# Untied differences of the gate weights, a place of its own for the first sums' split, spread puts, swapped PSUM pools and other turns of the late tiles in a float32 encoder layer

## Chip, cores and metric

One core of one Trainium2 chip runs the whole layer. The metric is the device time of one execution in microseconds (us). The engines are named as in the profile: PE is TensorE (matmul), DVE is VectorE, ACT is ScalarE, POOL is GpSimd, SP is SyncE, which issues most transfers (its queue shows as SPq).

## What is computed

A layer on 1024 tokens of width 1024, in float32, cut here to its skeleton:

```python
h = swiglu(rmsnorm(x, ffn1_pre_g), w_gate, w_up, w_down)      # 1024 -> 2816 -> 1024
x = x + 0.5 * rmsnorm(h, ffn1_post_g)
q, k, v = split(rmsnorm(x, mix_pre_g) @ w_qkv)                 # 16 heads of 64
o_na = neighbourhood_attention(q[:8], k[:8], v[:8], rel_bias)  # 2-D windows
o_dil = dilated_mixture_attention(q[8:], k[8:], v[8:], t5_bias)
mixed = concat(rmsnorm(o_na, na_out_g), rmsnorm(o_dil, dil_out_g)) @ w_out
x = x + rmsnorm(mixed, mix_post_g)
h = swiglu(rmsnorm(x, ffn2_pre_g), ...)                        # as above
x = x + 0.5 * rmsnorm(h, ffn2_post_g)
```

## The kernel before

**Products.** A float32 product is made of three matmuls on halves: `split` (L418 to L423) makes a high half on ACT (a cast, L421, names whi) and a low half on DVE (L422, wlo), and `mm3` (L325, L326, L327) multiplies high by high, high weight by low activation, low weight by high activation. Above that the large products follow a scheme with seven block products and pre-added operands: tiles are named A11, A12, A22 for plain quadrants and S1 to S4 for sums of the activations; T1, T2 and B22 are the weights' counterparts. One product of a block is four steps of three matmuls, 12 in all.

**Gate and up (`PairGemm`).** FFN 1 and FFN 2 each have 22 blocks of 128 columns; gate and up of a block form one such scheme. `ahead` first goes over the early blocks (9 in FFN 1, 10 in FFN 2) with the left half of the gate weights alone, while the last token tiles (4 to 7, the late tiles) are still normed, transposed and summed into S1 to S4; its results wait in DRAM. Then `run` takes all blocks in order. In an early block TensorE runs S2 with T2 (giving u2, L548), S1 with T1 (v, L556), S3 with T1 (c22, L575), S4 with B22, and one product later A22 with B22 (c21, L584). `prepare(b + 1)` gives the next block's weight work in four parts: `direct`, the differences on DVE (L510, L511, L512: first T1's pair, then T2, then B22's second); `second`, the split of T2; `sums`, the split of T1; `rest`, the split of B22 and the fetch of the block after (SP, L415 and L416). `begin` does `direct` and `second` for block 0 ahead of `run`, and `begin_rest` the others. The sink (`GatePairs`) applies silu and, after every second (odd) block, forms pair sums for the next product in four DVE operations (L647 to L650).

**Down, values.** `Passes` streams pairs of row blocks: raw tiles (praw, SP, L680 and L683), their halves (pw, L685 and L686), and the products accp. At the end of the last gate/up block, `final` closes the pools wg, tj and wt (T2's tiles) and opens on their space a pool for the first passes' four raw tiles. The q,k columns are a `PairGemm` with 8 blocks, all early, after the values' passes; its sink is `QKPairs`.

**Order.** TensorE's order is written out; on the other engines a scheduler orders by dependences and costs, except where `c.behind(f, engines)` ties what f issues behind the last instruction issued so far on those engines. Every engine works its own instructions in order. `plan` gives turns: `{1: [U(4)]}` has tile 4 put (transposed) from block 1's tick on.

**Other places.** Dilated heads read their queries regrouped by residue (`q_by_residue`, L978) and work scores (L1068, names sp), a fused add and sum on DVE (L989), exponentials on ACT (L991), transposes (L999) and values (L1089). The neighbourhood heads' output is normed in two quads of four token tiles (`scale`, L1237) and put: transposed by TensorE (L1248) and split (L1252, L1253), between the output projection's matmuls. `gemm_psum` opens the PSUM pools psm (6 banks of products) and pst (2 banks of transposes). A late tile runs through left_half and right_half (L260, L272 on ACT, L273 to L287 on DVE).

## Time and profile before

| what | before |
|---|---|
| median of three runs | 1915.44 us (1915.32 to 1922.39) |
| the profiled execution's own time | 1915.59 us |
| its span | 1913.4 us |
| TensorE busy | 1846.7 us, 97% |
| VectorE busy | 1331.3 us, 70% |
| ScalarE busy | 830.7 us, 43% |
| GpSimd busy | 318.7 us, 17% |
| mean granted TensorE clock | 0.993 |

Rows of the timeline give the start in us, the duration, the engine, line and operation, the tiles (out<-in, buffer numbers left out), the shape, and in brackets how long the engine stood idle before and what ended that. Rows of the waits give who waited for whom, then microseconds in all, times, and the longest. A transfer's landing is when its data is there, counted from its issue.

### The profile page before, as it was taken

Reading aid. Unit: us, or ns where it says so; the run is one execution under the profiler, and the core shown is the slowest. Engines: PE = TensorE matmul, PEld = TensorE weight load, DVE = VectorE, ACT = ScalarE, POOL = GpSimd, SP = SyncE. Lnnn points to the kernel's source line nnn. Section 1 sums busy time; section 2 is a strip of 40 time slices with the busy share of each in tenths; the row PEclk is TensorE's granted clock in tenths of the full one; section 3 lists DMA queues with packets and bytes.
Section 4 is the critical chain, followed back from the end, with each engine's and each line's share of the span. In section 5 each row is a group of like instructions: output and inputs, shape, how many; then the busy total and the mean of one; then the engine's idle time right before and its main releaser. Section 6 shows DMA issues by size and latency. Waiting matters only on the chain.

```text
span 1913.4 us, 25103 instructions
## 1 busy us (share of the span) xinstructions
PE 1846.7 (97%) x8904; PEld 1532.9 (80%) x8904; DVE 1331.3 (70%) x2233; ACT 830.7 (43%) x1491; POOL 318.7 (17%) x502
## 2 busy tenths in 40 slices
PE   7999999999999999899999999999999999999998
PEld 5777888888778877788899998877777888888886
DVE  6767777766565986467677756786768777654557
ACT  7422333334353656223588765563222333344333
POOL 2123111112210123122333100120101111110000
PEclk9999999999999999999999999999999999999999
DMA  7655565645996857757876432584546655476564
GB/s 264 220 182 192 166 237 209 227 158 201 342 330 197 287 194 257 253 165 236 281 234 224 166 136 89 183 307 143 174 151 231 218 194 210 157 267 217 195 227 146
DMA packets 171215, 404.94 MB, mean 212 GB/s; under 512 B 19841, under 2 KB 42273, under 8 KB 169042
## 3 DMA queue, kind: packets, MB, share of 16 engines
q1 hardware_dynamic: 123410, 243.18, 38.3%
q0 software_dynamic: 46672, 158.07, 22.9%
q10 hardware_dynamic: 1008, 2.10, 0.3%
q8 instruction: 70, 1.15, 0.2%
q14 instruction: 55, 0.45, 0.1%
HBM read 277.34 MB, written 130.99 MB: 213 GB/s over the span
## 4 chain that ended last, share of the span: by engine, by line
PE 64%; issue 16%; DVE 7%; DMA 6%; ACT 4%; POOL 2%; SPq 0%; DVEq 0%; POOLq 0%; ACTq 0%
PE mmp L327 11%; PE mmp L326 10%; PE mmp L325 10%; PE accp L326 8%; PE accp L327 8%; PE accp L325 8%; PE po L1089 2%; PE ptp L999 2%; PE po L1201 2%; DVE wlo L422 1%; PE sp L1068 1%; PE trp L157 1%; ACT whi L421 1%; PE sp L1185 1%; DVE pw L686 1%
## 5 line engine op out<-in xcount | busy, mean ns | idle before, releaser
L325 PE MATMUL mmp<-x,whi 128*128 128x512 f32 (+1 forms) x1464 | 579.9, 396 | 10.3 <-ACT whi L421 7.5
L327 PE MATMUL mmp<-x,wlo 128*128 128x512 f32 (+1 forms) x1464 | 576.9, 394 | 10.9 <-DVE wlo L422 10.9
L326 PE MATMUL mmp<-x,whi 128*128 128x512 f32 (+1 forms) x1464 | 574.9, 393 | 1.2 <-DVE x L244 0.7
L327 PEld LDWEIGHTS mmp<-x,wlo 128*128 128x128 f32 x1464 | 277.4, 189 | 76.5 <-DVE wlo L422 14.8
L325 PEld LDWEIGHTS mmp<-x,whi 128*128 128x128 f32 x1464 | 277.6, 190 | 74.2 <-ACT whi L421 12.0
L326 PEld LDWEIGHTS mmp<-x,whi 128*128 128x128 f32 x1464 | 277.4, 189 | 61.7 <-DVE x L244 1.0
L686 DVE TENSOR_TENSOR pw<-praw,pw 128x1024 fp32r<-128x1024 f32 (+1 forms) x181 | 201.6, 1158 | 128.8 <-ACT pw L685 128.5
L421 ACT CAST whi<-wraw 128x1024 fp32r<-128x1024 f32 x129 | 135.2, 1050 | 320.1 <-PE mmp L326 246.9
L685 ACT CAST pw<-praw 128x1024 fp32r<-128x1024 f32 (+1 forms) x181 | 168.9, 981 | 205.8 <-PE accp L327 144.6
L325 PE MATMUL accp<-pw 128*128 128x512 f32 x600 | 235.1, 392 | 2.1 <-ACT pw L685 1.1
L326 PE MATMUL accp<-pw 128*128 128x512 f32 x600 | 234.2, 390 | 1.8 <-DVE pw L686 1.8
L327 PE MATMUL accp<-pw 128*128 128x512 f32 x600 | 233.8, 390 | 0.0
L422 DVE TENSOR_TENSOR wlo<-wraw,whi 128x1024 fp32r<-128x1024 f32 x129 | 157.8, 1224 | 23.4 <-ACT whi L421 23.0
L325 PEld LDWEIGHTS accp<-pw 128*128 128x128 f32 x600 | 112.7, 188 | 27.5 <-ACT pw L685 2.4
L326 PEld LDWEIGHTS accp<-pw 128*128 128x128 f32 x600 | 112.7, 188 | 26.0 <-DVE pw L686 3.0
L327 PEld LDWEIGHTS accp<-pw 128*128 128x128 f32 x600 | 112.7, 188 | 23.2
L584 DVE TENSOR_TENSOR c<-mmp,u 128x512 f32<-128x512 f32 x52 | 36.0, 692 | 106.9 <-PE mmp L327 106.9
L630 POOL DMA_DIRECT2D g<-sg x44 | 23.9, 544 | 488.3 <-DVE sg L623 296.4
L440 ACT COPY s<-mmp 128x512 f32<-128x512 f32 x52 | 30.6, 588 | 127.1 <-PE mmp L327 118.6
L421 ACT CAST whi<-traw 128x512 fp32r<-128x512 f32 x52 | 32.3, 621 | 98.9 <-DVE traw L511 98.7
L510 DVE TENSOR_TENSOR wraw<-wraw 128x1024 f32<-128x1024 f32 x52 | 63.5, 1221 | 7.8 <-DMA wraw<-in_wqk_dram 7.0
L1201 PE MATMUL po<-vs,pt 128*128 128x128 f32 x352 | 50.1, 277 | 1.5 <-ACT pt L1001 1.1
(280 smaller groups left out, 2756.8 us busy)
## 6 DMA issues: line engine op xcount, KB each, us to landing
praw<-g SPq DMA_DIRECT2D x70, 512.0 KB, 5.6
wraw<-in_wg_dram SPq DMA_DIRECT2D x44, 512.0 KB, 4.2
wraw<-in_wu_dram SPq DMA_DIRECT2D x44, 512.0 KB, 6.0
tr<-in_wd_dram SPq DMA_DIRECT2D x44, 512.0 KB, 6.1
g<-sg POOLq DMA_DIRECT2D x88, 256.0 KB, 4.0
ts<-tr POOLq DMA_DIRECT2D x22, 1024.0 KB, 4.7
praw<-ts SPq DMA_DIRECT2D x88, 256.0 KB, 4.6
praw<-in_wd_dram SPq DMA_DIRECT2D x66, 256.0 KB, 5.3
```

The source lines that it names most:

```text
L325: nc.tensor.matmul(out, ahi, bhi, start=start, stop=False, skip_group_check=go_on)
L326: nc.tensor.matmul(out, ahi, blo, start=False, stop=False, skip_group_check=go_on)
L327: nc.tensor.matmul(out, alo, bhi, start=False, stop=stop, skip_group_check=go_on)
L421: nc.scalar.copy(hi, raw)
L422: nc.vector.tensor_sub(lo, raw, hi.bitcast(F32))
L510: nc.vector.tensor_sub(r[:, 0:2], r[:, 1:3], r[:, 0:2])
L584: nc.vector.tensor_add(c21, d, u2)
L685: nc.scalar.copy(hi, raw[:, :m])
L686: nc.vector.tensor_sub(lo, raw[:, :m], hi.bitcast(F32))
L999: nc.tensor.transpose(ps[:, j, :], src[:, j * P:(j + 1) * P], c.ident)
L1089: nc.tensor.matmul(po[:, un * 2 + j], pt[:, 2 * j + t, :], rhs, start=t == 0, stop=t == 1)
L1201: nc.tensor.matmul(po[0][:, u], pt[0][:, j, :], vs[:, k0 + j, :], start=j == 0, stop=j == n - 1)
```

## The change

It has these parts: `direct` is tied behind DVE only in `QKPairs` (`ties`), not in `GatePairs`; the split of T1 goes into the pool wt, and that of block 0 is issued in `begin` behind DVE and ACT, with the last early block's silu behind ACT; the q,k `begin` as a whole is issued behind DVE and ACT; the norm's squares of late tiles go behind ACT; the first pair of tiles in FFN 1's second half keeps its raw copy for later; the late tiles' turns in FFN 1 change; the first dilated head's queries are regrouped by ACT and not by GpSimd; the second quad of the neighbourhood heads is scaled tile by tile with the puts, and the eight puts stand at other distances between the matmuls; and FFN 2 opens pst ahead of psm.

```diff
     def norm(self, ts, xs):
-        n = self.squares(ts, xs)
+        n = []
+        self.c.behind(lambda: n.extend(self.squares(ts, xs)), ACT)
         self.c.sums.append(lambda: self.scale(*n))
...
+    def tied(self, f):
+        self.c.behind(f, *self.sink.ties)
...
         def sums():
-            w[T1] = self.split(r[:, 0:2, :], "m")
+            w[T1] = self.split(r[:, 0:2, :], "m", self.c.wt)
...
     def begin(self):
-        direct, second, *self.more = self.prepare(0)
+        direct, second, sums, *self.more = self.prepare(0)
         direct()
         second()
+        self.c.behind(sums, DVE, ACT)
...
-                c.behind(direct, DVE)
+                self.tied(direct)
                 second()
...
 class GatePairs:
+    ties = ()
...
-        nc.scalar.activation(sg, ps, AF.Silu)
+        c.behind(lambda: nc.scalar.activation(sg, ps, AF.Silu), *tie)
...
 class QKPairs:
+    ties = (DVE,)
...
-    def scale(self):
+    def scale(self, n=4):
...
+    def scaled(self, i):
+        o = self.og[:, self.b0 + i, :]
+        self.c.nc.vector.scalar_tensor_tensor(o, o, self.r[:, i:i + 1], self.gain, op0=ALU.mult, op1=ALU.mult)
...
-                        c.steps.extend(lambda t=t: op0.one(t) for t in (2 * b - 2, 2 * b - 1))
+                        c.steps.extend(lambda t=t: op0.one(t, *([keeps] if t > 1 else [])) for t in (2 * b - 2, 2 * b - 1))
...
-                                    {0: [F(4, 5), L(6, 7)], 1: [U(4), F(6, 7)], 2: [U(5)], 5: [U(6)], 6: [U(7)]},
+                                    {0: [F(4, 5), L(6, 7)], 1: [F(6, 7)], 2: [U(4)], 3: [U(5)], 4: [U(6)], 5: [U(7)]},
...
-            pg.begin()
+            c.behind(pg.begin, DVE, ACT)
...
-            c.behind(lambda: qs.append(q_by_residue(c, nc.gpsimd.tensor_copy, loaded[0][1])), POOL)
+            c.behind(lambda: qs.append(q_by_residue(c, nc.scalar.copy, loaded[0][1])), ACT)
...
+                    if quad and i < 3:
+                        puts.append(lambda i=i, n=n: (n.scaled(i + 1), n.put(i)))
+                    else:
+                        puts.append(lambda i=i, n=n: n.put(i))
...
-                    if t > 1 or k % 2:
-                        c.step()
+                    if t < 3 and (4 * t + k) % 3:
+                        puts.popleft()()
...
-            gemm_psum(ctx)
+            gemm_psum(ctx, ("pst", 2), ("psm", 6))
```

In the changed kernel all line numbers after the first hunk are higher (L510 is L514 there, L422 is L426, L685 is L692). DVE around an odd early block of FFN 1, before: c_1197 is the block's c22, s_1153 the first of the four pair sums of the pair before.

```order
L584 TENSOR_TENSOR c_1141<-mmp,u_1023 128x512
L422 TENSOR_TENSOR wlo<-wraw,whi 128x1024
L639 TENSOR_TENSOR c_1083<-c_1083,c_1141 128x512
L647 TENSOR_TENSOR s_1153<-c_983,c_1083 128x512
L556 TENSOR_TENSOR v<-mmp,u_1127 128x512
L648 TENSOR_TENSOR c_983<-sg,c_983 128x512
L649 TENSOR_TENSOR sg<-s_1153,sg 128x512
L650 TENSOR_TENSOR sg<-sg 128x512
L510 TENSOR_TENSOR wraw<-wraw 128x1024
L575 TENSOR_TENSOR c_1197<-mmp,v 128x512
L511 TENSOR_TENSOR traw<-wraw 128x512
```

The same engine in the changed kernel, from c22 of the block before (c_1083) to the same c21 (c_1141):

```order
L580 TENSOR_TENSOR c_1083<-mmp,v 128x512
L426 TENSOR_TENSOR wlo<-wraw,whi 128x1024
L514 TENSOR_TENSOR wraw<-wraw 128x1024
L635 TENSOR_TENSOR sg<-mmp,u_1023 128x512
L515 TENSOR_TENSOR traw<-wraw 128x512
L636 TENSOR_TENSOR sg<-sg,sgt 128x512
L516 TENSOR_TENSOR wraw<-wraw,traw 128x512
L553 TENSOR_TENSOR u_1127<-mmp,s_1112 128x512
L426 TENSOR_TENSOR wlo<-traw,whi 128x512
L589 TENSOR_TENSOR c_1141<-mmp,u_1023 128x512
```

The three differences and the low half of T2 have moved from behind the pair sums to ahead of u2 (u_1127) of the same block.

ACT at the end of FFN 1's gate and up, before; pw_3678 holds the down-projection's first halves, c_3708 is the last c21, and v belongs to the last block:

```order
L440 COPY u_3604<-mmp 128x512
L685 CAST pw_3678<-praw 128x1024
L609 ACTIVATE sg<-sg 128x512
L685 CAST pw_3678<-praw 128x1024
L440 COPY v<-mmp 128x512
L685 CAST pw_3679<-praw 128x1024
L685 CAST pw_3680<-praw 128x1024
L638 ACTIVATE c_3708<-c_3708 128x512
```

and in the changed kernel:

```order
L444 COPY u_3604<-mmp 128x512
L616 ACTIVATE sg<-sg 128x512
L444 COPY v<-mmp 128x512
L692 CAST pw_3678<-praw 128x1024 x2
L645 ACTIVATE c_3708<-c_3708 128x512
L692 CAST pw_3679<-praw 128x1024
L692 CAST pw_3680<-praw 128x1024
```

The first casts of the passes have moved behind v. DVE at the first late tile of FFN 2, in the changed kernel; trp_11477 is that tile's transposed right half, wraw_11768 the weights of block 1:

```order
L205 SCALAR_TENSOR_TENSOR x_11262<-x_11262,y_11415,gain_10678 128x1024
L426 TENSOR_TENSOR wlo_11452<-graw_11347,whi_11451 128x1024
L514 TENSOR_TENSOR wraw_11768<-wraw_11768 128x1024
L285 TENSOR_TENSOR s_11464<-s_11464,trp_11477 128x512
L287 TENSOR_TENSOR s_11464<-s_11464,x1_11357 128x512
L274 TENSOR_TENSOR x61_11232<-trp_11477,x60_11231 128x4x128
```

Before, the same rows stood without L514 (its place was at the very end of the part ahead, behind u2 of block 0).

More of the change, by code (lines that the diff above doesn't have):

```diff
@@ L486, in late @@
                 self.mm(a, w, 1, A12, s1 is None)
-                self.sink.first(b, a, True, *(() if s1 is None else (s1,)))
+                self.sink.first(b, a, True, s1, tie)
             c.tick()
@@ L490, in ahead @@
             c.behind(self.begin, DVE, ACT)
-        late()
+        late((ACT,) if ready else ())
     def save(self, b, a):
@@ L567, in run @@
                 self.sink.first(b, pb, False, s1)
-                c.behind(direct, DVE)
+                self.tied(direct)
                 second()
@@ L1230, in squares @@
             c.nc.scalar.activation(junk[:, :o.shape[-1]], o, AF.Square, accum_out=self.ss[:, i, part:part + 1])
-    def scale(self):
+    def scale(self, n=4):
         c = self.c
-        r = rstd_of(c, self.ss if self.ss.shape[2] == 2 else self.ss[:, :, 0], 512)
-        for i in range(4):
-            o = self.og[:, self.b0 + i, :]
-            c.nc.vector.scalar_tensor_tensor(o, o, r[:, i:i + 1], self.gain, op0=ALU.mult, op1=ALU.mult)
+        self.r = rstd_of(c, self.ss if self.ss.shape[2] == 2 else self.ss[:, :, 0], 512)
+        for i in range(n):
+            self.scaled(i)
+    def scaled(self, i):
+        o = self.og[:, self.b0 + i, :]
+        self.c.nc.vector.scalar_tensor_tensor(o, o, self.r[:, i:i + 1], self.gain, op0=ALU.mult, op1=ALU.mult)
     def put(self, i):
@@ L1264, in sub, with gemm_psum @@
             return ctx.enter_context(ExitStack())
-        def gemm_psum(stack):
-            c.psm = pool("psm", 6, stack, space=PSUM)
-            c.pst = pool("pst", 2, stack, space=PSUM)
+        def gemm_psum(stack, *names):
+            for n, b in names or (("psm", 6), ("pst", 2)):
+                setattr(c, n, pool(n, b, stack, space=PSUM))
         def ordered(*more):
@@ L1593, in begin @@
                     (lo0, lo1, lo2)[b](1)
+                while keeps:
+                    keeps.pop(0)()
                 pg.before = 2
@@ L1706, in last @@
             c.behind(lambda: n.squares(slice(448, 512), 1), ACT)
-            c.todo.append(lambda: c.behind(n.scale, DVE))
+            c.todo.append(lambda: c.behind(lambda: n.scale(1 if quad else 4), DVE))
         early = []
@@ L1751, in layer @@
             on = [c.xt.tile([P, 2, 4, T], F32R, tag=f"o{h}", name=f"n{h}") for h in (0, 2)]
-            for n in early:
+            puts = deque()
+            for quad, n in enumerate(early):
                 n.ot = on
-                c.steps.extend(lambda i=i, n=n: n.put(i) for i in range(4))
+                for i in range(4):
+                    if quad and i < 3:
+                        puts.append(lambda i=i, n=n: (n.scaled(i + 1), n.put(i)))
+                    else:
+                        puts.append(lambda i=i, n=n: n.put(i))
         s5.close()
```

8 lines of the change are left out of this document (4 added, 4 removed).

## The prediction

> **What bounds the kernel now.** I read the page's busy shares first, then the list of TensorE's waits, then the timeline of each stage in which a wait stands.
>
> ```profile
> span 1913.4 us, 25103 instructions
> PE 1846.7 (97%) x8904; PEld 1532.9 (80%) x8904; DVE 1331.3 (70%) x2233; ACT 830.7 (43%) x1491; POOL 318.7 (17%) x502
> ...
> PE mmp L327 <- DVE wlo L422: 10.9, 9, 2.6
> PE mmp L325 <- ACT whi L421: 7.5, 6, 2.2
> ```
>
> TensorE is the bound: busy for 97%, with few waits, and no other engine comes near. The change touches no matmul, so its price is the sum of the waits that it takes away less those that it puts in their place. The last two rows (microseconds in all, times, longest) are the largest groups: TensorE waiting for the high and the low half of a split weight. A wait in brackets in the rows below runs from a modelled end: matmuls of 512 columns show 0.39 us but start 0.23 apart (467.32 and 467.55, quoted further down), so a gap costs TensorE about 0.16 more than its bracket.
>
> **Differences of the early gate/up blocks (ties).** An odd early block of FFN 1: TensorE, then VectorE, then ScalarE's cast.
>
> ```profile
> 122.48 0.50 PE L325 MATMUL mmp<-x,whi 128*128 128x512 f32 x1 [1.03 <-ACT whi L421]
> 124.29 0.50 PE L327 MATMUL mmp<-x,wlo 128*128 128x512 f32 x1 [1.08 <-DVE wlo L422]
> ...
> 118.75 0.69 DVE L650 TENSOR_TENSOR sg<-sg 128x512 f32<-128x512 f32 x1
> 119.36 1.22 DVE L510 TENSOR_TENSOR wraw<-wraw 128x1024 f32<-128x1024 f32 x1
> 121.09 0.68 DVE L511 TENSOR_TENSOR traw<-wraw 128x512 f32<-128x512 f32 x1
> 121.81 1.22 DVE L422 TENSOR_TENSOR wlo<-wraw,whi 128x1024 fp32r<-128x1024 f32 x1
> ...
> 121.81 0.62 ACT L421 CAST whi<-traw 128x512 fp32r<-128x512 f32 x1
> ```
>
> L510 is tied behind the last VectorE instruction, which in an odd block is L650, the end of four pair sums. So T2's difference (L511) ends at 121.77, its cast starts at 121.81, and TensorE waits for both halves of T2. Untied, the first difference stands most of a block earlier (first excerpt in the section on the change), behind the low half of T1; both halves of T2 are then there long before TensorE comes. Which waits go: of the six in the cast's group one (2.2) belongs to the first sums below, which leaves 5.3; of the nine in the low half's group two (0.6 and 2.6), which leaves 7.7. That is 13.0 in 12 gaps; with 0.16 each **14.9 us**. What could be late next is what now stands behind the untied difference, u2 first: rival (4). From below the gain is nothing, if the waits only move.
>
> **First sums' split.** TensorE at the end of the part ahead of the blocks, FFN 1, then FFN 2:
>
> ```profile
> 80.36 0.50 PE L325 MATMUL mmp<-x,whi 128*128 128x512 f32 x1 [2.19 <-ACT whi L421]
> 81.70 0.50 PE L327 MATMUL mmp<-x,wlo 128*128 128x512 f32 x1 [0.61 <-DVE wlo L422]
> ...
> 1314.48 0.50 PE L327 MATMUL mmp<-x,wlo 128*128 128x512 f32 x1 [2.59 <-DVE wlo L422]
> ```
>
> T1 of block 0 takes a place that left weights still hold, and T2's cast stands behind it. In a place of its own, and issued in begin, it goes some microseconds earlier, beside matmuls: 2.19 + 0.61 + 2 x 0.16 = **3.1 us** in FFN 1, 2.59 + 0.16 = **2.75** in FFN 2; if the split is late all the same, nothing.
>
> **Begin of the q,k blocks behind VectorE and ScalarE.** TensorE, VectorE and ScalarE around 786:
>
> ```profile
> 784.04 0.47 PE L325 MATMUL accp<-pw,x 128*128 128x512 f32 x1 [0.83 <-DVE hb L736]
> 788.90 0.50 PE L325 MATMUL accp<-pw,x 128*128 128x512 f32 x1 [3.24 <-ACT pw L685]
> 790.35 0.80 PE L326 MATMUL accp<-pw,x 128*128 128x512 f32 x1 [0.95 <-DVE pw L686]
> ...
> 782.06 1.22 DVE L510 TENSOR_TENSOR wraw<-wraw 128x1024 f32<-128x1024 f32 x1 [7.02 <-DMA wraw<-in_wqk_dram]
> ...
> 786.86 1.04 ACT L421 CAST whi<-wraw 128x1024 fp32r<-128x1024 f32 x1 [1.72 <-DVE wraw L512]
> ```
>
> L510 holds VectorE 7.02 us for its weights, and T1's cast (L421) holds ScalarE ahead of the values' casts (L685), for which TensorE waits 3.24. Behind the queues none of them stands in front: 0.83 + 3.24 + 0.95 + 3 x 0.16 = 5.5. The q,k blocks come after the values' passes, so their splits lie beside matmuls; block 2's fetch, issued after them, comes later too, for which I take off 0.3: **5.2**, from 3 to 6.
>
> **What the new place costs.** The place makes the pool wt larger, and the raw tiles of the down-projection's first passes (L680, L683) come to lie on it. Their first load waited for the low half of T2; in the changed program it waits for the last reader of T1, the end of S3 in the last block. SP, VectorE, TensorE, and the landing of L683's loads issued from 442 to 446 and from 459 to 463:
>
> ```profile
> 442.85 0.38 SPq L680 DMA_DIRECT2D praw<-g  x1
> ...
> 462.07 0.69 DVE L575 TENSOR_TENSOR c<-mmp,v 128x512 f32<-128x512 f32 x1
> ...
> 467.32 0.39 PE L325 MATMUL accp<-pw 128*128 128x512 f32 x1
> 467.55 0.39 PE L326 MATMUL accp<-pw 128*128 128x512 f32 x1
> ...
> DMA to landing us min/median/max: 3.9/4.2/4.5
> ...
> DMA to landing us min/median/max: 4.4/6.5/7.2
> ```
>
> The load at 442.85 moves to about 461.9: L575 at 462.07 reads what S3 has finished. SP issues the loads behind it 0.4 to 0.5 apart, a dozen in a row as from 459 on, so the last row is the nearer one; the third, at 462.8, has 4.4 to 7.2 to land. I take 6.0 (it is early in the row): 468.8. A cast of 1.04 and a subtraction of 1.22 (786.86 and 121.81) make 471.1, against 467.55 for the matmul that needs it: **3.5 us**, from 1.9 to 4.7, in each feed-forward. In FFN 1 I let 0.8 come back where later passes wait for loads anyway: **-6.2** in all.
>
> **First dilated head's query copy on ScalarE.** GpSimd, VectorE, TensorE:
>
> ```profile
> 934.80 2.12 POOL L978 CAST q<-st 128x1024 fp32r<-128x1024 f32 x1
> ...
> 935.32 2.17 DVE L948 TENSOR_TENSOR qk<-qk 128x512 fp32r<-128x512 f32 x1 [1.40 <-ACT qk L947]
> 937.41 0.41 DVE L989 CUSTOM_DVE_ANT_1 s<-sp,g 128x256 f32<-128x256 f32 x1
> ...
> 938.22 0.51 PE L1068 MATMUL sp<-st 128*128 128x256 f32 x2 [3.52 <-DVE sa L989]
> ```
>
> L948 took 2.17 us, while a subtraction of this width takes 0.69 (118.75), and it ended with GpSimd's copy; L989, and TensorE's scores behind it, came after. On ScalarE the copy (about 1.04) runs beside L948 and ends before the first exponential can start: **+1.4**, between 0 and 2.
>
> **Scales and puts of the neighbourhood heads.**
>
> ```profile
> 1170.53 0.63 PE L1248 MATMUL trp<-ident,og 128*128 128x128 f32 x4 [0.75 <-DVE og L1237]
> 1180.52 0.63 PE L1248 MATMUL trp<-ident,og 128*128 128x128 f32 x4 [1.85 <-DVE n L1253]
> ```
>
> The first wait stays: four scales still stand in front of it. The second came from two puts whose low halves stood behind four scales in a row. With one scale per put I walk VectorE's rows to a wait of about 1.1 at the fifth put and little after: **+0.6** (-0.5 to +2).
>
> **Start of FFN 2.** TensorE, VectorE, and the landing of the load that SP issues at 1261.29:
>
> ```profile
> 1246.75 0.50 PE L325 MATMUL mmp<-x,whi 128*128 128x512 f32 x1 [1.36 <-ACT raw L238]
> 1283.77 0.41 PE L157 MATMUL trp<-ident,x 128*128 128x128 f32 x2 [1.25 <-DVE x L273]
> ...
> 1271.03 0.68 DVE L284 TENSOR_TENSOR s<-s,trp 128x512 f32<-128x512 f32 x1
> ...
> 1261.29 1.37 SPq L416 DMA_DIRECT2D wraw<-in_wu_dram  x1
> ...
> DMA to landing us min/median/max: 11.2/11.2/11.2
> ```
>
> With the pools swapped the first product no longer waits for the last transpose's reader; about 1 us is won at 1246.75. But the untied difference of block 1 now stands ahead of the first late tile's L284 (third excerpt) and waits for this load, until 1272.5. With its 1.22 L284 starts at 1273.7 instead of 1271.03. The new order of that tile's steps saves about 1.4 of these 2.7, so the next tile's chain, for which TensorE waits at 1283.77, is 1.3 late. It hangs on the load and not on TensorE, so the 1 us is eaten: **-1.3**, from -3 to +1.
>
> **Start of FFN 1.**
>
> ```profile
> 36.16 0.63 PE L157 MATMUL trp<-ident,xn 128*128 128x128 f32 x4 [3.08 <-DVE xn L204]
> ```
>
> The late tiles' turns, the keeps from PSUM and the squares behind ScalarE move this wait about. By the changed order I walk it to some 2.4 us here; about what is saved, here and at the small waits beside it, comes back at the third late tile, whose norm then stands behind more VectorE work: **0**, from -3 to +2.
>
> **The sum.** 14.9 + 3.1 + 2.75 + 5.2 - 6.2 + 1.4 + 0.6 - 1.3 + 0 = 20.5. Against the profiled run's 1915.6 (span 1913.4 and 2.2 around it), 0.15 above the median: **1895 us**.
>
> **The rivals.** (1) The ties' waits only move, to u2 or the next split, so that the ties don't do what they say. For it: VectorE works in order, and everything behind the difference slides. Against: T2 gains most of a block. The 14.9 are lost: 1910.
> (2) The loads onto the new place land like those at 442 to 446, 4.2 after issue: 467.0 + 1.04 + 1.22 = 469.3, a wait of 1.7 instead of 3.5, and 3.6 less in both: 1891. For it: one queue, and nothing else large on it. Against: the dozen loads in a row.
> The Trainium skill, "DMA: Bandwidth & Descriptors", section "Anatomy of one DMA — SWDGE (gpsimd) path", fits a transfer as 2.0 us plus its bytes by 436 GB/s; by that the first three loads, 1 MB together, would be there 4.4 us after 461.9, and the total come out at this rival's, by an estimate. The rows from 459 on disagree (6.5 for 256 KB).
> (3) The starts of both feed-forwards take the bad end of their bounds: 3 lost in FFN 1, 1.7 more in FFN 2: 1900.
> (4) Slower: the untied difference waits at the head of VectorE's queue for its fetch in every early block. The fetch, the low half after u2, and the landing of all L416 loads:
>
> ```profile
> 114.23 1.23 DVE L422 TENSOR_TENSOR wlo<-wraw,whi 128x1024 fp32r<-128x1024 f32 x1 [0.21 <-ACT whi L421]
> ...
> 116.08 0.59 SPq L416 DMA_DIRECT2D wraw<-in_wu_dram  x1
> ...
> DMA to landing us min/median/max: 4.5/6.0/12.3
> ```
>
> The fetch is issued at 116.08; the difference's new turn is behind the low half that ends at 123.03, so 6.9 are free. Behind it stand u2, c21 and the low half that here ends at 115.46; its product starts about 3.3 later, after two products of 12 matmuls. Up to some 10.2 us nothing is lost, and each microsecond more costs one in each of the 19 early blocks. From 11.3 on that is more than the 20.5 won; at the longest load, 12.3, the time is 1895 + 2.1 x 19 = 1935. For it: 11.2 at FFN 2's start. Against: a median of 6.0.
>
> **How the numbers follow.** Forecast 0.52, rival (1) 0.12, (2) 0.14, (3) 0.14, (4) 0.08. The range goes from 1885, which is (2) with the good ends of both starts and of the waits, to 1910, which is (1); only (4) and little else lie outside. About 0.5%, 9.6 us, is what a measurement of this kernel can tell from no change. Faster by more, below 1905.9, are the forecast, (2) and (3): 0.80. Within it is (1): 0.12. Slower is (4): 0.08.
>
> **What would show it.** Right: no wait on whi or wlo at the odd early blocks; a wait of 3 to 4 us on the pw halves at the first accp of each feed-forward, with the first praw load issued just after S3; none near 784 to 791; L948 near 0.69 us; the difference at FFN 2's start ending with a landing. Wrong: VectorE idle ahead of the differences in the early blocks, TensorE waiting on u2's bank there, or the first praw loads issued early.

## The result and the profile after

The changed kernel takes 1896.28 us (median of 4 runs, 1895.36 to 1899.5); the kernel before takes 1915.82 us on the same chip (1915.32 to 1922.39). The ratio is 0.9893, with a 95% interval from 0.9869 to 0.9918. The profiled execution took 1895.36 us with a span of 1893.6, that is 19.8 less than the span before, where the prediction's sum had 20.5.

The page of the changed kernel: span, busy time by engine, and the group of the first difference (L514, in the last column what VectorE waited for ahead of it):

```profile
span 1893.6 us, 25119 instructions
...
PE 1844.3 (97%) x8904; PEld 1528.4 (81%) x8904; DVE 1330.2 (70%) x2233; ACT 835.1 (44%) x1492; POOL 315.4 (17%) x501
...
L514 DVE TENSOR_TENSOR wraw<-wraw 128x1024 f32<-128x1024 f32 x52 | 63.5, 1222 | 11.3 <-DMA wraw<-in_wu_dram 10.2
```

TensorE's waits in the changed kernel (us in all, times, longest):

```profile
PE accp L327 <- DVE pw L693: 4.4, 7, 0.8
...
PE accp L326 <- ACT pw L692: 4.1, 3, 1.8
...
PE mmp L326 <- ACT whi L425: 2.9, 1, 2.9
...
PE mmp L328 <- DVE wlo L426: 1.3, 2, 0.9
```

The two groups on split weights, 18.4 us in 15 waits before, are down to 4.2 in 3. In FFN 1 and FFN 2 no wait on a whi or wlo is left where `run` works an early block. One odd early block shows how, VectorE first, then ScalarE, then TensorE:

```profile
117.83 1.21 DVE L426 TENSOR_TENSOR wlo<-wraw,whi 128x1024 fp32r<-128x1024 f32 x1
120.14 1.23 DVE L514 TENSOR_TENSOR wraw<-wraw 128x1024 f32<-128x1024 f32 x1 [1.10 <-DMA wraw<-in_wu_dram]
...
121.89 0.68 DVE L515 TENSOR_TENSOR traw<-wraw 128x512 f32<-128x512 f32 x1
...
122.68 0.62 ACT L425 CAST whi<-traw 128x512 fp32r<-128x512 f32 x1 [5.02 <-DVE traw L515]
...
133.18 0.39 PE L326 MATMUL mmp<-x,whi 128*128 128x512 f32 x1
```

The difference stands behind the low half of T1 and waits 1.10 us for its fetch, at the head of VectorE's queue, as rival (4) feared; but T2's cast is over at 123.3, ten microseconds before TensorE comes for it at 133.18. Over the whole kernel VectorE spends 10.2 us in such waits, and TensorE none.

To see where the 19.8 us came from, I worked three sums out of the start times of all TensorE instructions of each profile. **Waits**: how much longer than usual for its shape it is from one instruction's start to the next, where that is over 0.24 us. **Half clock**: 512-column matmuls that start 0.40 to 0.44 apart where 0.23 is usual. **Pitch**: what the other 512-column matmuls take above 227 ns each. The few tenths that are missing lie in the smaller shapes.

| us | waits | half clock | pitch | span |
|---|---|---|---|---|
| before | 65.2 | 8.2 | 22.0 | 1913.4 |
| after | 45.2 | 2.8 | 27.5 | 1893.6 |
| difference | -20.0 | -5.4 | +5.6 | -19.8 |

The prediction spoke of waits alone. It gave them 20.5 and they gave 20.0. The two other rows were not in it, and that they cancel is luck.

### The profile page after: what moved, and what is told of

It reads as the page before. It is cut to its first block, busy times and chain, and to the rows that moved or that the text cites. A ratio compares the mean times of both kernels' runs of the same rounds, so it can differ in the third digit from the quotient of the medians.

```text
span 1893.6 us, 25119 instructions
## 1 busy us (share of the span) xinstructions
PE 1844.3 (97%) x8904; PEld 1528.4 (81%) x8904; DVE 1330.2 (70%) x2233; ACT 835.1 (44%) x1492; POOL 315.4 (17%) x501
## 4 chain that ended last, share of the span: by engine, by line
PE 81%; DMA 7%; DVE 6%; issue 3%; ACT 3%; POOL 1%; SPq 0%; DVEq 0%; ACTq 0%; POOLq 0%
PE mmp L328 16%; PE mmp L326 16%; PE mmp L327 16%; PE accp L327 8%; PE accp L328 8%; PE accp L326 7%; PE po L1098 2%; PE ptp L1008 2%; PE po L1210 2%; DMA praw<-in_wd_dram 1%; PE sp L1077 1%; PE sp L1194 1%; DVE pw L693 1%; PE trp L157 1%; DMA tr<-in_wv_dram 1%
## 5 line engine op out<-in xcount | busy, mean ns | idle before, releaser
L692 ACT CAST pw<-praw 128x1024 fp32r<-128x1024 f32 (+1 forms) x181 | 170.4, 983 | 227.9 <-PE accp L328 155.6
L425 ACT CAST whi<-wraw 128x1024 fp32r<-128x1024 f32 x129 | 135.2, 1051 | 236.8 <-PE mmp L327 233.0
L426 DVE TENSOR_TENSOR wlo<-wraw,whi 128x1024 fp32r<-128x1024 f32 x129 | 157.5, 1223 | 19.8 <-ACT whi L425 19.6
L589 DVE TENSOR_TENSOR c<-mmp,u 128x512 f32<-128x512 f32 x52 | 35.9, 690 | 85.5 <-PE mmp L328 85.3
L514 DVE TENSOR_TENSOR wraw<-wraw 128x1024 f32<-128x1024 f32 x52 | 63.5, 1222 | 11.3 <-DMA wraw<-in_wu_dram 10.2
L580 DVE TENSOR_TENSOR c<-mmp,v 128x512 f32<-128x512 f32 x52 | 35.8, 688 | 31.8 <-PE mmp L328 30.6
```

The costliest lines, as they stand in the source:

```text
L425: nc.scalar.copy(hi, raw)
L426: nc.vector.tensor_sub(lo, raw, hi.bitcast(F32))
L514: nc.vector.tensor_sub(r[:, 0:2], r[:, 1:3], r[:, 0:2])
L589: nc.vector.tensor_add(c21, d, u2)
L692: nc.scalar.copy(hi, raw[:, :m])
```

## The experiments

The ratios below are against the kernel before, measured beside each of them; its median was 1915.1 to 1916.9 us. Besides the medians, I read each profile at the stage that the edit concerns, since single executions of one kernel lie 0.2 to 0.6% apart (1895.36 to 1899.5 us for the changed kernel, 1909.79 to 1920.85 for the kernel before).

### The ties alone

```diff
 (kernel before)
-                c.behind(direct, DVE)
+                self.tied(direct)      # GatePairs: no tie; QKPairs: DVE
```

> The kernel before with one part of the change: the gate blocks' differences untied, those of q,k tied as before. Theory A (the tie alone made T2's halves late): the 12 waits on whi and wlo at the odd early blocks go, 15.6 us counted start to start, and the untied difference costs up to 2 at the start of FFN 2 as in the changed kernel: 1900 to 1902 us. Rival (the waits only move to u2 or the next split, and another part of the change took them away): 1912 to 1916 us with new waits in the odd early blocks.

Measured: 1894.72 us (1893.89 to 1896.82), ratio 0.9894, 0.9875 to 0.9913. TensorE's waits on the halves of split weights in this kernel:

```profile
PE mmp L325 <- ACT whi L424: 3.7, 2, 2.2
...
PE mmp L327 <- DVE wlo L425: 1.1, 2, 0.6
```

Both theories expected too little. The waits that went are those of the early blocks; over the whole kernel the sum of the waits fell by 15.0, where the prediction had 14.9 for this part. The rest is outside the waits: half clock fell by 3.2 us and pitch by 1.6. So the ties alone do what the whole change does. The other parts together are worth nothing, which the section on the first sums' old place shows to be a gain and a loss that cancel.

### The old ties back in the changed kernel

```diff
 (changed kernel)
 class GatePairs:
-    ties = ()
+    ties = (DVE,)
```

> The changed kernel with the old ties back in both FFNs (a tie of each difference behind the last VectorE instruction, as in q,k), everything else of the change kept. Theory A: the ties are the change's whole gain, with or without the other parts; the waits at the odd early blocks come back (15.6 us in the two FFNs, 1.2 us each before a whi and before a wlo), the stretches at half clock that follow some of them with them, and the time is 1911 to 1917 us, that of the kernel before. Rival: with the first sums ahead in their own place the ties cost less, since what they delay is no longer the first split of each block, and the time is 1900 to 1908 us.

Measured: 1916.99 us (1913.97 to 1922.52), ratio 1.001, 0.9996 to 1.0024. TensorE in the same odd early block:

```profile
119.80 0.50 PE L326 MATMUL mmp<-x,whi 128*128 128x512 f32 x1 [0.86 <-ACT whi L425]
121.62 0.50 PE L328 MATMUL mmp<-x,wlo 128*128 128x512 f32 x1 [1.09 <-DVE wlo L426]
```

Theory A held: the two waits of an odd early block are back with about their old sizes, and the time is that of the kernel before, though all other parts of the change are still there. From both sides the ties are the gain.

### The first sums in their old place

```diff
 (changed kernel)
-            w[T1] = self.split(r[:, 0:2, :], "m", self.c.wt)
+            w[T1] = self.split(r[:, 0:2, :], "m")
...
-        direct, second, sums, *self.more = self.prepare(0)
+        direct, second, *self.more = self.prepare(0)
...
-        self.c.behind(sums, DVE, ACT)
```

> The changed kernel, but the first block's sums are split where they were before (the places of the other splits, in their old turn), everything else kept. Theory A, from the stalls read in the traces: the waits for down sums at the ends of both FFNs (3.0 and 2.2 us) go, 1.5 us of waits in the later passes of FFN 1 come back, and the waits at the first sums of both FFNs (3.1 and 2.8 us; 3.1 and 2.3 in the run with the ties alone) come back: the part nets about 2 us, so this kernel is about 2 us slower than the changed one, 1897 to 1900 us. Rival: the place costs as much as it brings or more, and the kernel is as fast as the changed one or up to 3 us faster, 1893 to 1896.5.

Measured: 1887.37 us (1885.62 to 1888.3), ratio 0.9848, 0.9834 to 0.9861: 9 us faster than the changed kernel. Theory A fell, and the rival, right in direction, allowed 3 us at most. What the waits say is as expected, but for the later passes of FFN 1, which take 1.8 us less instead of waiting 1.5 more. SP's first load of the down-projection in this kernel, then in the changed one with the waits of TensorE behind it:

```profile
436.24 0.38 SPq L686 DMA_DIRECT2D praw<-g  x1
```

```profile
455.46 0.38 SPq L687 DMA_DIRECT2D praw<-g  x1
...
462.90 0.51 PE L326 MATMUL accp<-pw 128*128 128x512 f32 x1 [1.81 <-ACT pw L692]
464.16 0.50 PE L327 MATMUL accp<-pw 128*128 128x512 f32 x1 [0.75 <-DVE pw L693]
```

Here the first load goes out 19 us earlier, and no wait stands at the first accp; at the first sums of FFN 1 and FFN 2 the waits are back. The surprise is in the pitch, 21.5 us, near the 22.0 of the kernel before, instead of 27.5. The last twelve matmuls that use one T1, first the changed kernel's (its first matmul, and the first of the next product), then this one's:

```profile
277.17 0.40 PE L326 MATMUL mmp<-x,whi 128*128 128x512 f32 x1
...
279.97 0.39 PE L326 MATMUL mmp<-x,whi 128*128 128x512 f32 x1
```

```profile
278.29 0.39 PE L326 MATMUL mmp<-x,whi 128*128 128x512 f32 x1
...
281.01 0.39 PE L326 MATMUL mmp<-x,whi 128*128 128x512 f32 x1
```

It is the same product of the same block, with no wait in it: 2.80 us against 2.72. Over both feed-forwards, T1's matmuls start 233.1 ns apart on average in the changed kernel and 227.6 in this one, with the same moving rows. At 5.5 ns each, the 1,056 matmuls that the T1 of the 44 blocks have (24 a block) cost 5.8 us, and from the kernel before to the changed one the pitch rose by 5.6.

### The other split in the new place

```diff
 (kernel with the sums in their old place)
-            w[B22] = self.split(r[:, 2:4, :], "n")
+            w[B22] = self.split(r[:, 2:4, :], "n", self.c.wt)
```

> The kernel with the sums in their old place, but the other split of every block (the one for S4 and A22, of the same size) goes into the new place instead. Theory A: the place itself makes a product slower, some 233 ns instead of 227 ns from one matmul to the next, whichever weights lie there: FFN 1's late blocks (from 245 to 445 us) lose about 2.5 us against the kernel before as the changed kernel's do, and the FFN ends wait as there or longer, since the last reader of the place is now the last product of all: 1895 to 1903 us. Rival: it was the early split of the sums, not the place, that slowed those blocks: they take what they take with the sums in their old place, and the time stays under 1893 us.

Measured: 1915.03 us (1913.04 to 1917.93), ratio 0.9998, 0.9983 to 1.0014. TensorE in this kernel at the end of FFN 1 and in its first passes:

```profile
471.39 0.79 PE L326 MATMUL accp<-pw 128*128 128x512 f32 x1 [8.01 <-ACT pw L691]
...
492.63 0.79 PE L326 MATMUL accp<-pw 128*128 128x512 f32 x1 [6.00 <-ACT pw L691]
```

Theory A was right in kind on both counts, too high in size on the first and far too low on the second. The matmuls that stand from 245 to 445 us in the kernel before (the late blocks) take 1.2 us longer here than there (1.5 in the changed kernel, nothing with the sums in their old place), and B22's matmuls start 233.0 ns apart instead of 227.9, while T1's are back at 228.1. Other weights lie in the place and no split is earlier: the place sets the pitch. And the loads now wait for the last product of all, A22 (the first is issued at 463.22, where the changed kernel has 455.46), so TensorE waits 8.01 us where the changed kernel had 1.81, and in FFN 1 another 6.00 at 492.63. Here the last reader of the place has moved back by two products, some 5.5 us, and the seam of the two stages pays it in full.

### Only block 0's sums ahead, and the fetch behind the load

```diff
 (kernel with the sums in their old place)
+            if b == 0 and self.sink.first_apart:      # GatePairs only
+                m = self.c.tj.tile([P, 4, T], F32R, tag="r", name="wm")
+                w[T1] = hi, lo = m[:, 0:2], m[:, 2:4]
+                nc.scalar.copy(hi, r[:, 0:2, :])
+                nc.vector.tensor_sub(lo, r[:, 0:2, :], hi.bitcast(F32))
...
+        if self.sink.first_apart:
+            self.c.behind(self.more.pop(0), DVE, ACT)
```

> The kernel with the sums in their old place (1887.4 us), but the split of the first block's sums alone goes ahead, into the buffer that the down sums use later; from block 1 on nothing differs from it. Theory A: the new place was worth its 5.5 us at the first sums of both FFNs and cost what it cost (the ends of both FFNs, and 6 ns more for each of the 1056 products with those sums) only because all 22 blocks of an FFN use it; so the waits at 83.92 (1.5 us), 1297.49 and 1298.75 (2.3) go, nothing comes back, and the time is 3 to 5 us less: 1882.5 to 1884.5. Rival: what TensorE no longer waits for there it waits for at the next product, and the time stays at 1886 to 1888.5.

Measured: 1882.3 us (1880.67 to 1884.48), ratio 0.9826, 0.9807 to 0.9845. Theory A held: the waits at the first sums are gone, and nothing came back at the ends of the feed-forwards or in the pitch (20.3 us), since only one block in 22 uses the other place. The second kernel adds the tie of a fetch behind a load on SP, which the next section takes by itself:

> As the run before, and in the q,k stage the fetch of block 2 behind the load of block 0's kept sum. Theory A: the wait at 817.14 in the kernel with the sums in their old place (1.5 us) goes as the one of 3.0 us did in the changed kernel: 1 to 1.5 us less than the run before, 1881 to 1883. Rival: that wait has another cause here, since the sums are split later: within 0.7 us of the run before.

Measured: 1880.88 us (1878.81 to 1881.81, 5 runs), ratio 0.9815, 0.9797 to 0.9834. Theory A held here too: the matmuls that stand from 816 to 844 us in the kernel before lose 0.3 us here and 3.8 in the kernel without the tie (2.1 of wait and 1.6 of half clock behind it). The medians differ by 1.4 us. This is the best version I found, 34 us below the kernel before and 15 below the changed one.

### The q,k stage: load before fetch

```diff
 (changed kernel; first try)
         def rest():
             w[B22] = self.split(r[:, 2:4, :], "n")
-            self.fetch(b + 2)
+            if b or not self.sink.load_first:         # QKPairs only
+                self.fetch(b + 2)
...
                 nc.sync.dma_start(s1, self.kept[b])
+                if b == 0 and self.sink.load_first:
+                    self.fetch(2)
```

> The changed kernel, but block 2's weights of the q,k stage are fetched behind the load of block 0's kept s1 and not ahead of it. Theory A (the new 3.0 us wait near 825 comes from s1's load, which lands 7.6 us after its issue because the fetch of 1 MB and the values' stores were issued just ahead of it; u2 and, tied behind u2, T2's difference of block 1 follow it): s1 lands about 4 us after its issue, u2 comes about 3 us earlier, the wait at S2 of block 1 falls below 0.5: 1893 to 1894 us; the fetch lands later but is needed 13 us on. Rival (the load is slow by the values' stores alone, or the tie alone decides): the wait stays above 2 us, 1895.5 to 1896.5 us.

Measured: 1899.67 us (1896.58 to 1902.53), ratio 0.9913, 0.989 to 0.9936, and the wait at 828 was still 2.72. This tells nothing of either theory, since the edit did not do what it says. But the queue's order is that of the changed kernel, and still the median is 3.4 us higher; differences of this size between other kernels here prove nothing by themselves. SP's queue in its profile:

```profile
815.21 0.55 SPq L419 DMA_DIRECT2D wraw<-in_wqk_dram  x1
815.79 0.61 SPq L420 DMA_DIRECT2D wraw<-in_wqk_dram  x1
817.65 0.80 SPq L550 DMA_DIRECT2D s<-s1d  x2
```

The fetch still goes out first, since the order in a queue is settled by what is ready, and the load waits for a place that the values' passes hold to their end. The second try ties the fetch behind the load in SP's own queue:

```diff
-                    self.fetch(2)
+                    c.behind(lambda: self.fetch(2), SP)
```

> The changed kernel, but the q,k stage's fetch of block 2 is tied behind the load of block 0's kept sum in SP's own queue, so that it is issued after that load (in the run before this one the edit left the order of SP's queue as it was: the fetch was still issued 2.4 us ahead of the load). Theory A: the new wait of 3.0 us at 824.88 us of the changed kernel is there because the kept sum lands 7.6 us after its issue, behind the fetch's 512 KB, instead of 3.7 us as in the kernel before; issued first, it lands in about 4 us, the wait falls under 0.5 us and the time is about 2.7 us less than the changed kernel's, 1893 to 1894 us. Rival: the tied difference itself stands too late behind that load's addition on VectorE, and TensorE waits for it however soon the load lands: the wait stays above 2 us and the time within 1 us of the changed kernel's.

Measured: 1895.02 us (1893.7 to 1898.5, 5 runs), ratio 0.9892, 0.9877 to 0.9906. The changed kernel first (SP, the landing of the load issued at 813.90, VectorE, ScalarE, TensorE), then this one (SP, the landing of the load issued at 814.17, VectorE):

```profile
811.46 0.55 SPq L419 DMA_DIRECT2D wraw<-in_wqk_dram  x1
...
813.90 8.72 SPq L549 DMA_DIRECT2D s<-s1d  x3
...
DMA to landing us min/median/max: 7.6/7.6/7.6
...
821.59 0.69 DVE L553 TENSOR_TENSOR u<-mmp,s 128x512 f32<-128x512 f32 x1 [6.99 <-DMA s<-s1d]
...
824.24 0.62 ACT L425 CAST whi<-traw 128x512 fp32r<-128x512 f32 x1 [14.65 <-DVE traw L515]
...
824.88 0.47 PE L326 MATMUL mmp<-x,whi 128*128 128x512 f32 x1 [2.85 <-ACT whi L425]
```

```profile
814.17 0.32 SPq L550 DMA_DIRECT2D s<-s1d  x1
814.53 0.55 SPq L419 DMA_DIRECT2D wraw<-in_wqk_dram  x1
...
DMA to landing us min/median/max: 4.0/4.0/4.0
...
818.28 0.69 DVE L556 TENSOR_TENSOR u<-mmp,s 128x512 f32<-128x512 f32 x1 [3.41 <-DMA s<-s1d]
```

In the changed kernel the load of 256 KB lands 7.6 us after its issue, behind a fetch issued 2.4 us ahead; u2 (L553) waits for it, the tied difference stands behind u2, and the cast for which TensorE waits behind that. Issued first, the load lands in 4.0 and TensorE does not wait. Theory A held at this place: the stage is 2.9 us shorter. The median fell by 1.3 us only, which is within the scatter; in this profile other waits (the starts of both feed-forwards and FFN 1's first passes) are longer.

### No ties at all

```diff
 (changed kernel)
 class QKPairs:
-    ties = (DVE,)
+    ties = ()
```

> The changed kernel without the ties in the q,k stage as well. Theory A: in q,k the fetched weights lie there long before, so a tie buys nothing that shows but the order of VectorE's queue; without it the differences of block 1 run as soon as the first block's are done, ahead of the addition that waits for the kept sum, and the wait of 3.0 us at 824.88 goes: 1893 to 1894.5 us. Rival 4 of the prediction, seen from here: an untied difference stands at the head of VectorE's queue while its fetch is under way, and what is queued behind it waits, so that waits of several us appear in the q,k stage between 825 and 905 us: 1898 to 1905 us.

Measured: 1902.6 us (1899.42 to 1903.23), ratio 0.9925, 0.9913 to 0.9938. VectorE and TensorE in the values' last passes, and TensorE in the q,k stage:

```profile
784.59 1.23 DVE L514 TENSOR_TENSOR wraw<-wraw 128x1024 f32<-128x1024 f32 x1 [8.06 <-DMA wraw<-in_wqk_dram]
...
786.93 1.22 DVE L693 TENSOR_TENSOR pw<-praw,pw 128x1024 fp32r<-128x1024 f32 x1
...
788.20 0.50 PE L327 MATMUL accp<-pw,x 128*128 128x512 f32 x1 [2.66 <-DVE pw L693]
...
828.79 0.47 PE L326 MATMUL mmp<-x,whi 128*128 128x512 f32 x1 [1.09 <-DVE v L561]
```

Each theory was right in part. The wait of 2.85 at 824.88 is 1.09, as theory A had it. But the differences now stand among the values' passes, at the head of VectorE's queue, 8.06 us ahead of their weights; the value sums and the low half that TensorE needs stand behind, and it waits 2.66. This is rival (4)'s mechanism, at 786 instead of after 825. Its profile is 7.2 us longer than the changed kernel's, and the matmuls that stand from 764 to 925 us there explain about 1.2 of them. Most of the rest lies at the ends of FFN 1 (1.7) and FFN 2 (1.7) and in the attention (1.5), which the edit does not touch, with 2.4 us more of half clock among it; no experiment shows the cause.

### Which buffer the first passes load into

```diff
 (changed kernel)
-                q = pool("praw", 4, r, side="right")
-                raws = [q.tile([P, 2, T], F32, tag="x", name="praw") for _ in range(4)]
+                q = pool("praw", 1, r, side="right")
+                raws = [q.tile([P, 2, T], F32, tag=f"x{i}", name="praw") for i in range(4)]
+                raws = [raws[i] for i in (2, 3, 0, 1)]
```

> The changed kernel, with the first two of the four raw tiles of the down-projection's first passes laid on the space of tj and not on that of T1 (the later two lie on T1). Theory A (the load waits for T1's last reader in S3, and that alone makes the first halves late): the loads of the first weights are issued some 18 us earlier, the waits at the first accp of both feed-forwards go (3.0 and 2.2 us), of which about 1 is lost again at the later passes of FFN 1: 1891.5 to 1893 us. Rival (the dozen loads in a row, or the place of the halves, bind the first product anyway): the first accp still waits over 1.5 us, 1895 to 1896.5 us.

Measured: 1895.11 us (1894.48 to 1897.09), ratio 0.9896, 0.9878 to 0.9915: the rival's range. VectorE and TensorE at the end of FFN 1:

```profile
460.78 0.69 DVE L589 TENSOR_TENSOR c<-mmp,u 128x512 f32<-128x512 f32 x1 [0.90 <-PE mmp L328]
461.39 1.22 DVE L693 TENSOR_TENSOR pw<-praw,pw 128x1024 fp32r<-128x1024 f32 x1
...
462.66 0.50 PE L327 MATMUL accp<-pw 128*128 128x512 f32 x1 [1.68 <-DVE pw L693]
```

The wait for the cast is gone, since the first loads no longer lie on the new place. But the low half stands behind the last c21 (L589), which waits for TensorE's last product, and 0.69 + 1.22 later TensorE gets it. So an early load alone takes away little more than a third of this wait (3.0 to 1.85 us in FFN 1), and then a later pass (at 495.85) waits 1.5 us longer.

### The query copy on GpSimd, and the old turns

```diff
 (changed kernel, first kernel)
-            c.behind(lambda: qs.append(q_by_residue(c, nc.scalar.copy, loaded[0][1])), ACT)
+            c.behind(lambda: qs.append(q_by_residue(c, nc.gpsimd.tensor_copy, loaded[0][1])), POOL)
```

> The changed kernel with the first dilated head's query copy on GpSimd again. Theory A (the copy takes 2.0 us on ScalarE, so that it delays the exponentials by about 1 and gives back most of what VectorE's shorter subtraction won): the wait at the scores is 3.5 again instead of 2.05 and that at the first values' product 0.3 instead of 1.0: 0.3 us slower than the changed kernel, within noise. Rival (the 1.4 us forecast were won and something else lost 1.1): 1.4 us slower, with both waits as long as in the two kernels' worse case.

Measured: 1899.38 us (1895.93 to 1901.57), ratio 0.9915, 0.9894 to 0.9936. VectorE, ScalarE and TensorE in this kernel, then in the changed one:

```profile
930.05 2.16 DVE L957 TENSOR_TENSOR qk<-qk 128x512 fp32r<-128x512 f32 x1 [1.40 <-ACT qk L956]
...
932.59 0.76 ACT L1000 ACTIVATE pb<-s,sa 128x256 f32<-128x256 f32 x1 [2.57 <-DVE sa L998]
...
932.96 0.74 PE L1077 MATMUL sp<-st 128*128 128x256 f32 x4 [3.51 <-DVE sa L998]
```

```profile
927.95 0.69 DVE L957 TENSOR_TENSOR qk<-qk 128x512 fp32r<-128x512 f32 x1 [1.40 <-ACT qk L956]
...
927.82 2.03 ACT L987 CAST q<-st 128x1024 fp32r<-128x1024 f32 x1
929.75 0.75 ACT L1000 ACTIVATE pb<-s,sa 128x256 f32<-128x256 f32 x1
...
929.38 1.04 PE L1077 MATMUL sp<-st 128*128 128x256 f32 x4 [2.05 <-DVE sa L998]
...
936.19 1.05 PE L1098 MATMUL po<-va,pt 128*128 128x128 f32 x7 [1.02 <-ACT pt L1010]
```

The move does what the prediction says of L957 (2.16 to 0.69) and of TensorE's wait (3.51 to 2.05). But the copy takes 2.03 us on ScalarE, the first exponential (L1000) starts behind it, and the values' product that needs it waits 1.02. TensorE's waits are as theory A had them, 0.3 us apart in sum. By the clock more is left: the first exponential starts 2.54 us behind L957's start here, as in the kernel before, and 1.80 in the changed kernel, and from the first score matmul to that values' product it is 11.29 us here and in the kernel before, and 10.53 in the changed one. So the copy on ScalarE is worth about 0.75 us at this place. The rest of the 3 us between the medians lies elsewhere: this profile has 6.6 us of half clock against 2.8.

```diff
 (changed kernel, second kernel)
-                                    {0: [F(4, 5), L(6, 7)], 1: [F(6, 7)], 2: [U(4)], 3: [U(5)], 4: [U(6)], 5: [U(7)]},
+                                    {0: [F(4, 5), L(6, 7)], 1: [U(4), F(6, 7)], 2: [U(5)], 5: [U(6)], 6: [U(7)]},
```

> The changed kernel with the late tiles' old turns in FFN 1 (put of tile 4 ahead of the norm of tiles 6 and 7, the puts of 6 and 7 three turns later). Theory A: the new waits of TensorE at 53.70 us (1.6, for a late tile's normalised rows) and 72.43 us (1.1, for a low half) come with the new turns; with the old ones they go, FFN 1's start costs 5.6 us as before instead of 6.6 and the time is about 1 us less than the changed kernel's: 1895 to 1896. Rival: those waits come from the norm that is no longer tied as a whole behind ScalarE, and stay with the old turns: 1896 to 1897 us.

Measured: 1899.44 us (1897.06 to 1902.37), ratio 0.9913, 0.9897 to 0.9928. Its wait on a late tile's normalised rows:

```profile
PE trp L157 <- DVE xn L205: 4.5, 1, 4.5
```

The two waits are indeed gone, but one of 4.5 us stands in place of one of 2.0. From 31 to 85 us the stage is 0.35 shorter than in the changed kernel, which is too little to tell. The median is higher, and again the profile differs by half clock most of all (6.7 against 2.8). That part stays undecided.

## Why the prediction was right

The time was forecast to 1.3 us, but in part by luck: the sum of waits was right, two terms that I left out cancelled, and within the sum errors of 4.1 us one way and 4.6 the other (the table below) cancelled too. The step that failed is the first conclusion: "The change touches no matmul, so its price is the sum of the waits that it takes away less those that it puts in their place". The matmuls' own time changed by -5.4 us of half clock and +5.6 of pitch; had only one of them moved, the time would have been 1891 or 1902.

By its steps, in us of waits:

| step | forecast | measured |
|---|---|---|
| ties at the early blocks | 14.9 | 15.6 (5.2 and 10.4) |
| first sums, FFN 1 and FFN 2 | 3.1, 2.75 | 3.1, 2.8 |
| begin of q,k | 5.2 | 3.0 |
| new place at the ends of both FFNs | -6.2 | -3.8 |
| query copy | 1.4 | 0.3 |
| neighbourhood puts | 0.6 | 1.0 |
| start of FFN 2 | -1.3 | -0.7 |
| start of FFN 1 | 0 | -1.0 |
| small ones elsewhere | | -0.3 |
| sum | 20.5 | 20.0 |

**Ties.** Right in mechanism and size, shown from both sides. The margin was there too: the median landing of L420 is 6.1 us, under the 10.2 that the working gave as free. One of the signs that I had named for being wrong, VectorE idle ahead of the differences, did show (the 10.2 us of waits above); it was a poor sign, since those waits cost TensorE nothing.

**First sums.** Right to a tenth.

**Begin of q,k.** The 6.0 us at 784 to 791 went as said. I took off 0.3 for block 2's fetch, which "comes later too"; in fact B22's split moved ahead with the others, so the fetch went out before the kept sum's load instead of long after it, and cost 3.0. The step lacked SP's order at this place, and the run with the tie on SP shows that this was all of it.

**New place.** The waits are 3.0 and 2.2 instead of 3.5 twice: the third load landed 5.4 us after its issue, not 6.0. The 1.45 that came back in later passes are not the place's doing, as I had it: with the ties alone these passes also wait 2.1 less, and with the sums in their old place 2.8. What the step did not have are the slower matmuls, 5.8 us, which made the place cost more than all its waits. Had it been forecast rightly, the advice would have been to leave this part out.

**Query copy.** Mis-sized: I took 1.04 for the copy on ScalarE, from a cast of 128x1024 that reads and writes in order (the page still has 1051 ns for those); this one reads by residue and takes 2.03. The 0.3 in the table is what TensorE's waits show; by the starts of the rows about 0.75 was won.

**The starts.** Within their bounds. In FFN 1 the walk had 2.4 us for the first wait on a late tile and it was 2.0; what came back at later tiles, 1.4 at 53.70 and 0.9 at 72.43, was a little more than what was saved.

**The rivals.** (1) fell: nothing that stands behind the difference was late. (2) was half true, with landings of 4.0 and 5.4 for the first and the third load. By the fit in the Trainium skill, "DMA: Bandwidth & Descriptors", section "Anatomy of one DMA — SWDGE (gpsimd) path", which is for transfers that GpSimd issues, those three loads would by an estimate be there 4.4 us after the first issue; issued by SP, they were there 6.3 after it (455.46 to 461.78), so the trace stays slower than the page. (3) came to 0.4 of its 4.7. (4) did not come in the feed-forwards, and its mechanism shows in the run without any tie.

## What to carry to other kernels

An order tie behind an engine's last instruction is priced by when that instruction ends; ask for the landing times before taking one away, and put a tie only on the queue whose order matters (the load and the fetch on SP). When a buffer moves, ask three things: who reads it last and what will be loaded onto it next, how many matmuls read their weights from it, and whether all blocks need the new place or only the first. A sum of waits that fits the measured time is no proof: split the difference by waits, clock and time per matmul before believing it.

## What the hardware did that I had not expected

**Half clock after short waits.** TensorE's granted clock falls to half for some 3.4 us after some waits that are far shorter than that. In the kernel before, such stretches start at 82.76, 154.44, 789.32 (twice as long), 939.50, 1314.97 and 1413.96 us; in the changed kernel at 38.74, 465.41 and 929.62. Those at 939.50 and 929.62 lie in the attention, without 512-column matmuls, so the sum above does not count them. Rows of windows give start and end, length, busy times of PE, PEld, DVE, ACT and POOL with their instructions, then PEclk (the granted clock as a share of full speed), the DMA share and GB/s. First the kernel before, ahead of the stretch at 1413.96 and in it; the two waits of an odd early block of FFN 2 end at 1412.54 and 1414.36, so the second had only begun:

```profile
1410.55:1413.96 3.41, 1.71 (x7) 0.77 (x5) 3.37 (x6) 1.67 (x2) 0.00 (x0) 1.00 1.01 399
1413.96:1417.37 3.41, 3.01 (x7) 2.43 (x8) 1.64 (x3) 0.00 (x0) 0.54 (x1) 0.50 0.29 83
```

Then the changed kernel, behind its waits at 462.90 and 464.16, and around the longer one that ends at 824.88, which no half clock follows:

```profile
465.41:468.82 3.41, 3.41 (x9) 2.63 (x8) 2.81 (x4) 1.25 (x2) 1.51 (x4) 0.50 1.04 401
...
820.40:823.81 3.41, 1.63 (x8) 1.01 (x6) 2.19 (x3) 0.00 (x0) 0.00 (x0) 1.00 0.37 120
823.81:827.22 3.41, 2.34 (x10) 1.97 (x11) 3.41 (x6) 2.22 (x3) 0.00 (x0) 1.00 0.17 64
```

Each stretch costs 0.8 to 1.6 us on its 512-column matmuls (the long one 2.4), on top of the wait, and no view of waits shows it: the matmuls count as busy. Between the profiles of the variants this sum ran from 0 to 8.2 us, which is a good part of their scatter. Within a profile the stretches start whole multiples of 3.413 us apart (154.44 is 21 of them behind 82.76, 1413.96 is 390; 465.41 is 125 behind 38.74). So it matters where a wait falls on this beat: the wait that ends at 824.88 began at 822.03, and the beat cuts it at 823.81. The Trainium skill, "TensorE: Matmul & The Clock Gate", section "What's actually happening", says that the clock is halved after at least one idle window of about 3.4 us, in windows that run freely. The length, the half rate and the beat agree with these rows; the condition doesn't, for the window ahead of 1413.96 was not idle: seven matmuls were in it. In every profile with such a stretch I also counted how much of each window its matmuls fill, start to start and with 0.227 us at most for one of 512 columns. No window that was filled above 0.41 was followed by half clock; the one ahead of 1413.96 has 0.38, the one from 820.40 has 0.43. Some emptier ones, most of them in the attention, were not followed by it either, so what decides it in full no run here settles.

**The pitch of a matmul depends on where its weights lie.** Matmuls with weights in the new place took 233 ns from start to start and in the old one 227.6 (T1) or 227.9 (B22), with the same moving operand, whichever weights lay there. T2, which always lies in that pool, showed 233 before as well, and in the q,k stage, where the pool lies elsewhere, T1 and T2 showed 226.7. The weights' place is not all of it: the left weights of the late blocks lie in the same pool as T1 in its old place, and their matmuls, with other moving rows, took 233.5. I did not find the rule behind it.

**VectorE beside GpSimd.** L957 took 2.16 us beside GpSimd's copy and 0.69 beside ScalarE's, in the rows above. The Trainium skill, "SBUF — State Buffer", section "SBUF: two separate sides", has it that VectorE with two SBUF inputs and a GpSimd instruction that reads SBUF hold a shared pair of ports by turns; the two rows agree.
